# A decoder step of windowed attention, gated linear attention and SwiGLU: mixed tiles kept in DRAM as single values, and split where the output projection reads them

## The chip, the core and the metric

The kernel runs on one core of a Trainium2 chip. The metric is the device time of one execution in microseconds (us); lower is better. The core's engines are TensorE (PE in the profile; PEld is its weight load), VectorE (DVE), ScalarE (ACT), GpSimd (POOL) and SyncE (SP). DMAs are issued by SP's queue and by POOL's.

## The reference, cut to what matters

2048 prompt tokens and 8 decode tokens of width 1024 go through one layer in float32:

```python
def finish(x, o_attn, o_gla, r_gla, gla_norm_g, w_o, ffn_norm_g, w_gate, w_up, w_down):
    g = rmsnorm(o_gla, gla_norm_g).reshape(N, T, GLA_WIDTH) * jax.nn.silu(r_gla)
    h = x + jnp.concatenate([o_attn, g], axis=-1) @ w_o
    z = rmsnorm(h, ffn_norm_g)
    return h + (jax.nn.silu(z @ w_gate) * (z @ w_up)) @ w_down
```

`o_attn` (512 columns) is the sliding-window attention with sinks, `o_gla` (512 columns) the gated linear attention. Their concatenation is what the kernel calls the mixed tile: 128 tokens by 1024 columns, 16 tiles.

## The kernel before

Products are exact to nearly float32: an operand is split into a high part (rounded to fp32r by ACT, line 91) and a low part (the rest, a subtraction, line 92), and `mm3` issues three matmuls (lines 103 to 105): high times high, high times low, low times high. `split` is the helper for both steps; its last argument moves the subtraction from DVE to another engine.

The work runs in five stages, one behind the other, and the tile framework orders the instructions of each engine by a simulated timeline; every engine then works through its own list strictly in order.

- Attention, about 0 to 415 us. For each of 16 blocks of 128 tokens `front`, `project`, `project_r` and `attend` make the normalised input, the projections and the attention output `o` [128, 512], transposed. At the end of `attend` (lines 390 to 392) `o` is split into `mo`, the high part on ACT, the low part on POOL, and SP stores both (512 KB) into `mix_d[b]`.
- Linear attention, about 415 to 755 us. For each pair of blocks `front_b` projects and `gla_b` runs the recurrence. At its end (lines 861 to 864) ACT scales the transposed result `ps_m` by the gain into the high part of `mob`, DVE makes the low part, and SP stores 512 KB into the other half of `mix_d[b]`. `mob` has one buffer.
- Output stage, about 755 to 990 us. Eight pieces of the output weights are loaded as `wro` into a ring of four buffers (tag `raw`, pool `c_raw`) and split into `WO`. Then for each tile `product` (lines 962 to 983) loads the mixed tile, both parts, straight into `mt` (1 MB, two buffers), and the residual row block into `h`; 48 matmuls (2 halves, 8 k, 3 each) make `ps_wo`, DVE adds them to `h` (line 576), SP stores `h`. `normalise` squares `h` on ACT, scales it on DVE into `z` (line 992), TensorE transposes `z` (8 transposes, line 997). After two tiles `operands` makes seven units (b and t and their differences), each split on ACT and DVE into `zhl`, which has three buffers, and stored by POOL's queue to `zc_d` (line 1017, 512 KB each). Tiles go 0, 4, 1, 5, 2, 6, 3, 7, 8, 12, ..., the decode tile third from last; in the text "the second tile" is the second of this list. While the first tiles run, the `raw` ring also takes the first weights of the next stage (`wrg`), which are split into `whl`.
- Gate and up products (about 1000 to 1879 us) and down products (to 2340 us), each in a two-level Strassen form.

The rings of two to four buffers tie the engines together: a unit may be cast into `zhl` only when the store three units earlier has landed, a `wro` load waits until the split of the load four earlier is done, and SP's queue starts its DMAs in order, so one that waits holds those behind it.

Of the kernel before, what the change touches and what calls it, by code (L numbers as in the profile page):

```python
# [20 lines left out]
P = 128  # L21
# [30 lines left out]
def hymba_kernel(ctx: ExitStack, tc: tile.TileContext, I, O, X=None, phases=3):  # L52
# [11 lines left out]
    nT_d = [dram.tile([P, 2, KD, 256], F32, name=f"nT_d{i}") for i in range(NB // 2)]  # L64
    mix_d = [dram.tile([P, 2, KD, P], F32, name=f"mix_d{i}") for i in range(NB)]
    lr_d = [dram.tile([16, 256], F32, name=f"lr_d{i}") for i in range(NB // 2)]
# [76 lines left out]
    with ExitStack() as ph:  # L143
# [192 lines left out]
        def attend(b):  # L336
# [36 lines left out]
            kts = (1,) if b == 0 else (0, 1)  # L373
            o = wl.tile([P, 512], F32, tag="o", name="o", bufs=1)
            ol = wl.tile([P, 512], F32, tag="ol", name="ol", bufs=1)
            lo, hi = slice(0, 64), slice(64, 128)
            for v, (rh, rl) in enumerate(((lo, hi), (hi, lo))):
# [11 lines left out]
                nc.vector.tensor_tensor(o[rh], po[rh], ol[rh], ALU.add)  # L389
            mo = wl.tile([P, 2, 512], F32R, tag="mo", name="mo", bufs=1)  # L390
            split(mo[:, 0], mo[:, 1], o, nc.gpsimd)
            nc.sync.dma_start(mix_d[b][:, :, 0:4, :], mo.bitcast(F32).rearrange("p s (c t) -> p s c t", c=4))

# [188 lines left out]
    with ExitStack() as ph:  # L582
# [166 lines left out]
        def gla_b(pp):  # L749
# [68 lines left out]
            for c in range(2):  # L818
# [39 lines left out]
                for hh in range(4):  # L858
                    hc = slice(hh * P, (hh + 1) * P)
                    nc.tensor.transpose(ps[:, hc], ob[:, hc], ident)  # L860
                mo = wl.tile([P, 2, 512], F32R, tag="mo", name="mob", bufs=1)
                nc.scalar.activation(mo[:, 0], ps, AF.Copy, scale=gg)
                nc.vector.scalar_tensor_tensor(mo[:, 1], ps, gg, mo[:, 0].bitcast(F32), ALU.mult, ALU.subtract)
                nc.sync.dma_start(mix_d[b][:, :, 4:8, :], mo.bitcast(F32).rearrange("p s (c t) -> p s c t", c=4))

# [73 lines left out]
    with ExitStack() as ph:  # L939
# [21 lines left out]

        def product(ti):
            n = P if ti < NB else ND
            h = hp.tile([P, D], F32, tag="h", name="h")
            if ti < NB:
                mt = mixp.tile([P, 2, KD, P], F32R, tag="mix", name="mt")
                nc.sync.dma_start(mt.bitcast(F32), mix_d[ti])
                nc.sync.dma_start(h, I["x_prompt"][0, ti * P:(ti + 1) * P, :])
            else:
                nc.sync.dma_start(h[:n], I["x_sample"].rearrange("n o d -> (n o) d"))  # L970
            for dh in range(2):
                cols = slice(dh * 512, dh * 512 + 512)
                ps = acc.tile([P, 512], F32, tag="acc", name="ps_wo")
                for k in range(KD):
                    if ti < NB:
                        mm3(ps, mt[:, 0, k], mt[:, 1, k], WO[:, 0, k, cols], WO[:, 1, k, cols], k == 0, k == KD - 1)
                    else:
                        for hl in range(2):
                            nc.tensor.matmul(ps[:40], mixdec[:, k], WO[:, hl, k, cols], start=k == 0 and hl == 0,
                                             stop=k == KD - 1 and hl == 1)  # L980
                add_h(h, n, dh, ps)
            nc.sync.dma_start(h_d[ti] if ti < NB else hdec_d, h[:n])
            return h
# [39 lines left out]
        def after(ti):  # L1023
# [5 lines left out]
            if j == 1:  # L1029
                operands(sb, mt, bs.pop((sb, mt)))  # L1030

        for i, ti in enumerate(tiles):
            if ti == NB or (ti % 8 < 4 and (ti // 8, ti % 4) not in bs):
                key = (1, 3) if ti == NB else (ti // 8, ti % 4)
                bs[key] = [bp.tile([P, 4, 132], F32, tag=f"b{q}", name=f"b{q}", bufs=2) for q in range(4)]
            hs[ti] = product(ti)
            if i:
                after(tiles[i - 1])
# [317 lines left out]
```

## Time and profile before

| | |
|---|---|
| median of 3 runs | 2338.44 us (2336.45 to 2340.04) |
| the profiled execution | 2342.2 us, span 2340.4 us |
| busy share of the span | PE 95%, PEld 82%, DVE 68%, ACT 40%, POOL 27% |
| mean granted TensorE clock | 0.975 |
| DMA | 364.56 MB, mean 156 GB/s |
| the chain that ended last | PE 70%, DVE 8%, DMA 8%, issue 7%, POOL 4%, ACT 2% |

A busy PE is a modelled figure: each matmul's record is longer than the distance to the next, so a PE without gaps in the timeline is at its pace, whatever the sum of the records. "Idle before" names what the engine waited for last. The chain of waits goes back from the last instruction, at each step to what released it.

### The profile page before, as it was taken

The page shows a single profiled execution, that of the slowest core. Times are in us where ns is not written, and L with a number is a line of the kernel's source. Part 1 is how long each engine was busy: PE and PEld are TensorE (multiplying, and loading weights), DVE is VectorE, ACT ScalarE, POOL GpSimd, SP SyncE. Part 2 cuts the span into 40 slices and gives each one's busy share as a digit, 9 for nine tenths or more (in the row PEclk, how much of TensorE's full clock was granted, in tenths as well). Part 3 has the DMA queues.
Part 4 walks back from the last instruction along what each step waited for, and adds up shares of the span by engine and source line. Part 5 has one row for each costly group of instructions (what it writes and reads, how often), then busy time and mean ns, then how long its engine had stood idle before and what let it go on. Part 6 is the DMA issues. An engine that isn't in the chain of part 4 may idle for free.

```text
span 2340.4 us, 34821 instructions
## 1 busy us (share of the span) xinstructions
PE 2229.1 (95%) x12649; PEld 1923.1 (82%) x12649; DVE 1589.9 (68%) x3236; ACT 946.7 (40%) x2120; POOL 629.6 (27%) x807
## 2 busy tenths in 40 slices
PE   8899998999996999589999999999999989999998
PEld 6788887788885788478888889999999958787887
DVE  6687887587876655546666666767666674848477
ACT  5667877343433332223323233333333243534342
POOL 2444544364463122301101010101111112222222
PEclk9999999899997999799999999999999999999999
DMA  6323435243222899773333338323333357878877
GB/s 218 122 91 113 132 107 167 87 145 105 91 82 85 259 323 307 243 285 122 112 91 110 93 111 345 109 91 100 96 95 109 129 156 176 211 166 212 191 177 267
DMA packets 204571, 364.56 MB, mean 156 GB/s; under 512 B 15063, under 2 KB 127968, under 8 KB 198368
## 3 DMA queue, kind: packets, MB, share of 16 engines
q1 hardware_dynamic: 167376, 258.79, 34.3%
q0 software_dynamic: 37024, 103.55, 17.2%
q8 instruction: 100, 1.64, 0.3%
q14 instruction: 71, 0.58, 0.1%
HBM read 211.08 MB, written 152.27 MB: 155 GB/s over the span
## 4 chain that ended last, share of the span: by engine, by line
PE 70%; DVE 8%; DMA 8%; issue 7%; POOL 4%; ACT 2%; SPq 0%; POOLq 0%; ACTq 0%; DVEq 0%
PE ps_b L104 7%; PE ps_b L103 7%; PE ps_b L105 7%; PE ps_a L103 5%; PE ps_c L104 5%; PE ps_a L104 5%; PE ps_a L105 5%; PE ps_c L103 5%; PE ps_c L105 5%; DMA zc_d_P<-zhl 4%; PE ps_d L103 3%; PE ps_d L104 3%; PE ps_d L105 3%; POOL bd L776 1%; DMA wr<-in_w_in_dram 1%
## 5 line engine op out<-in xcount | busy, mean ns | idle before, releaser
L104 PE MATMUL ps_b<-z,whl 128*128 128x258 f32 (+1 forms) x792 | 253.4, 320 | 0.0
L103 PE MATMUL ps_b<-z,whl 128*128 128x258 f32 (+1 forms) x792 | 253.1, 320 | 0.0
L105 PE MATMUL ps_b<-z,whl 128*128 128x258 f32 (+1 forms) x792 | 252.2, 318 | 0.0
L103 PE MATMUL ps_a<-z,whl 128*128 128x258 f32 (+1 forms) x528 | 170.0, 322 | 26.0 <-DMA z<-zc_d_P 26.0
L91 ACT CAST dm<-mr 128x384 fp32r<-128x384 f32 (+1 forms) x224 | 107.8, 488 | 180.3 <-PE ps_b L105 95.8
L104 PE MATMUL ps_a<-z,whl 128*128 128x258 f32 (+1 forms) x528 | 170.1, 322 | 0.0
L105 PE MATMUL ps_a<-z,whl 128*128 128x258 f32 (+1 forms) x528 | 169.8, 322 | 0.0
L104 PE MATMUL ps_c<-z,whl 128*128 128x258 f32 (+1 forms) x528 | 169.1, 320 | 0.0
L105 PE MATMUL ps_c<-z,whl 128*128 128x258 f32 (+1 forms) x528 | 168.9, 320 | 0.0
L103 PE MATMUL ps_c<-z,whl 128*128 128x258 f32 (+1 forms) x528 | 168.5, 319 | 0.0
L105 PEld LDWEIGHTS ps_b<-z,whl 128*128 128x128 f32 x792 | 148.8, 188 | 12.0
L103 PEld LDWEIGHTS ps_b<-z,whl 128*128 128x128 f32 x792 | 148.9, 188 | 11.8
L104 PEld LDWEIGHTS ps_b<-z,whl 128*128 128x128 f32 x792 | 148.8, 188 | 11.8
L92 DVE TENSOR_TENSOR dm<-mr,dm 128x384 fp32r<-128x384 f32 (+1 forms) x224 | 114.7, 518 | 64.2 <-ACT dm L91 64.2
L91 ACT CAST whl<-wrg 128x512 fp32r<-128x512 f32 x132 | 81.6, 620 | 151.2 <-PE ps_b L105 83.1
L776 POOL TENSOR_TENSOR bd<-E,qTb 64x128 f32<-64x128 f32 x224 | 120.8, 539 | 66.1 <-ACT E L764 52.6
L103 PEld LDWEIGHTS ps_a<-z,whl 128*128 128x128 f32 x528 | 100.4, 190 | 34.6 <-DMA z<-zc_d_P 26.5
L1194 POOL DMA_DIRECT2D md_d<-m x22 | 15.6, 710 | 391.8 <-DVE m L1157 378.7
L936 DVE TENSOR_TENSOR gu<-ps_c,gu 128x512 f32<-128x512 f32 (+1 forms) x130 | 77.8, 599 | 56.1 <-PE ps_c L105 55.5
L92 DVE TENSOR_TENSOR whl<-wrg,whl 128x512 fp32r<-128x512 f32 x132 | 90.9, 689 | 35.2 <-ACT whl L91 34.9
L103 PE MATMUL ps_wo<-WO,mt 128*128 128x512 f32 x256 | 102.7, 403 | 9.4 <-ACT WO L91 9.4
L104 PEld LDWEIGHTS ps_a<-z,whl 128*128 128x128 f32 x528 | 100.1, 190 | 8.1
(386 smaller groups left out, 6617.5 us busy)
## 6 DMA issues: line engine op xcount, KB each, us to landing
mr<-md_d SPq DMA_DIRECT2D x24, 1344.0 KB
zc_d_P<-zhl POOLq DMA_DIRECT2D x49, 512.0 KB, 8.1
wrg<-in_w_gate_dram SPq DMA_DIRECT2D x44, 512.0 KB
wrg<-in_w_up_dram SPq DMA_DIRECT2D x44, 512.0 KB
nT_d<-nT SPq DMA_DIRECT2D x16, 1024.0 KB
zT<-nT_d SPq DMA_DIRECT2D x8, 2048.0 KB
mt<-mix_d SPq DMA_DIRECT2D x16, 1024.0 KB
z<-zc_d_P SPq DMA_DIRECT2D x7, 2064.0 KB
```

The source lines that it names most:

```text
L91: nc.scalar.copy(h, src)
L92: (eng or nc.vector).tensor_tensor(l, src, h.bitcast(F32), ALU.subtract)
L103: nc.tensor.matmul(ps, lh, rh, start=start, stop=False, skip_group_check=more)
L104: nc.tensor.matmul(ps, lh, rl, start=False, stop=False, skip_group_check=more)
L105: nc.tensor.matmul(ps, ll, rh, start=False, stop=stop, skip_group_check=more)
L776: nc.gpsimd.tensor_tensor(bv[rows, :, h], eo, qo, ALU.mult)
L936: nc.vector.tensor_tensor(out, a, b, ALU.add)
L1194: nc.gpsimd.dma_start(md_d[sb][g][:, :, q, fp - GROUPS[g][0], :], src.rearrange("p (m t) -> p m t", m=4))
```

## The change

The mixed tiles are stored as single float32 values. `mix_d[b]` has half the size. In the attention stage the split of `o` is gone, `o` has two buffers, and SP stores it as it is (256 KB). In the linear-attention stage ACT's scaled copy is the tile itself, VectorE's low part is gone, `mob` has two buffers of half the size. In the output stage `load_tile` loads a tile (512 KB) into a buffer `mr` of the `raw` ring and splits it into `mt` with ACT and DVE; it is called one tile ahead of the product.

```diff
--- before.py
+++ after.py
@@ -62,7 +62,7 @@
 
     ext_d = dram.tile([8, 384], F32, name="ext_d")
     nT_d = [dram.tile([P, 2, KD, 256], F32, name=f"nT_d{i}") for i in range(NB // 2)]
-    mix_d = [dram.tile([P, 2, KD, P], F32, name=f"mix_d{i}") for i in range(NB)]
+    mix_d = [dram.tile([P, KD, P], F32, name=f"mix_d{i}") for i in range(NB)]
     lr_d = [dram.tile([16, 256], F32, name=f"lr_d{i}") for i in range(NB // 2)]
     vdec_d = dram.tile([ND, 512], F32, name="vdec_d")
     rdec_d = dram.tile([ND, 512], F32, name="rdec_d")
@@ -371,7 +371,7 @@
                 nc.gpsimd.tensor_tensor(St[:, :, k0:], St[:, :, k0:],
                                         den[:, hs].unsqueeze(2).to_broadcast([P, 4, nk]), ALU.mult)
             kts = (1,) if b == 0 else (0, 1)
-            o = wl.tile([P, 512], F32, tag="o", name="o", bufs=1)
+            o = wl.tile([P, 512], F32, tag="o", name="o", bufs=2)
             ol = wl.tile([P, 512], F32, tag="ol", name="ol", bufs=1)
             lo, hi = slice(0, 64), slice(64, 128)
             for v, (rh, rl) in enumerate(((lo, hi), (hi, lo))):
@@ -387,9 +387,7 @@
                     nc.tensor.matmul(po, vv[:, v], pT[:, 1], start=False, stop=kt == 1)
                 nc.scalar.copy(ol[rh], po[rl])
                 nc.vector.tensor_tensor(o[rh], po[rh], ol[rh], ALU.add)
-            mo = wl.tile([P, 2, 512], F32R, tag="mo", name="mo", bufs=1)
-            split(mo[:, 0], mo[:, 1], o, nc.gpsimd)
-            nc.sync.dma_start(mix_d[b][:, :, 0:4, :], mo.bitcast(F32).rearrange("p s (c t) -> p s c t", c=4))
+            nc.sync.dma_start(mix_d[b][:, 0:4, :], o.rearrange("p (c t) -> p c t", c=4))
 
         def decode_a():
             with ExitStack() as decs:
@@ -858,10 +856,9 @@
                 for hh in range(4):
                     hc = slice(hh * P, (hh + 1) * P)
                     nc.tensor.transpose(ps[:, hc], ob[:, hc], ident)
-                mo = wl.tile([P, 2, 512], F32R, tag="mo", name="mob", bufs=1)
-                nc.scalar.activation(mo[:, 0], ps, AF.Copy, scale=gg)
-                nc.vector.scalar_tensor_tensor(mo[:, 1], ps, gg, mo[:, 0].bitcast(F32), ALU.mult, ALU.subtract)
-                nc.sync.dma_start(mix_d[b][:, :, 4:8, :], mo.bitcast(F32).rearrange("p s (c t) -> p s c t", c=4))
+                mo = wl.tile([P, 512], F32, tag="mo", name="mob", bufs=2)
+                nc.scalar.activation(mo, ps, AF.Copy, scale=gg)
+                nc.sync.dma_start(mix_d[b][:, 4:8, :], mo.rearrange("p (c t) -> p c t", c=4))
 
         def decode_b():
             a = dp.tile([P, 2, ND], F32, name="a")
@@ -959,15 +956,20 @@
             if dh == 0:
                 nc.sync.dma_start(gBf, bcast_rows(I["ffn_norm_g"], D))
 
-        def product(ti):
+        def load_tile(ti):
+            h = hp.tile([P, D], F32, tag="h", name="h")
+            if ti == NB:
+                nc.sync.dma_start(h[:ND], I["x_sample"].rearrange("n o d -> (n o) d"))
+                return None, h
+            mr = craw.tile([P, 1024], F32, tag="raw", name="mr").rearrange("p (k t) -> p k t", k=KD)
+            nc.sync.dma_start(mr, mix_d[ti])
+            mt = mixp.tile([P, 2, KD, P], F32R, tag="mix", name="mt")
+            split(mt[:, 0], mt[:, 1], mr)
+            nc.sync.dma_start(h, I["x_prompt"][0, ti * P:(ti + 1) * P, :])
+            return mt, h
+
+        def product(ti, mt, h):
             n = P if ti < NB else ND
-            h = hp.tile([P, D], F32, tag="h", name="h")
-            if ti < NB:
-                mt = mixp.tile([P, 2, KD, P], F32R, tag="mix", name="mt")
-                nc.sync.dma_start(mt.bitcast(F32), mix_d[ti])
-                nc.sync.dma_start(h, I["x_prompt"][0, ti * P:(ti + 1) * P, :])
-            else:
-                nc.sync.dma_start(h[:n], I["x_sample"].rearrange("n o d -> (n o) d"))
             for dh in range(2):
                 cols = slice(dh * 512, dh * 512 + 512)
                 ps = acc.tile([P, 512], F32, tag="acc", name="ps_wo")
@@ -1029,11 +1031,15 @@
             if j == 1:
                 operands(sb, mt, bs.pop((sb, mt)))
 
+        ready = load_tile(tiles[0])
         for i, ti in enumerate(tiles):
             if ti == NB or (ti % 8 < 4 and (ti // 8, ti % 4) not in bs):
                 key = (1, 3) if ti == NB else (ti // 8, ti % 4)
                 bs[key] = [bp.tile([P, 4, 132], F32, tag=f"b{q}", name=f"b{q}", bufs=2) for q in range(4)]
-            hs[ti] = product(ti)
+            now = ready
+            if i + 1 < len(tiles):
+                ready = load_tile(tiles[i + 1])
+            hs[ti] = product(ti, *now)
             if i:
                 after(tiles[i - 1])
         after(tiles[-1])
```

The order of the instructions on ACT where the output stage begins, before (`mob` is the last mixed tile, `wro` a piece of the output weights, `whl` a unit of the next stage's weights, line 990 the square of `h`):

```order
L862 ACTIVATE mob<-ps_m,gg 128x512
L91 CAST WO<-wro 128x2x512 x8
L91 CAST whl<-wrg 128x512 x2
L91 CAST whl<-sy 128x512 x2
L91 CAST whl<-wrg 128x512 x2
L91 CAST whl<-sx 128x512
L990 ACTIVATE z,ss<-h 128x1024 x2
L1000 COPY b_8522<-ps_zT 128x4x128
```

and now:

```order
L860 ACTIVATE mob<-ps_m,gg 128x512
L91 CAST WO<-wro 128x2x512 x8
L91 CAST mt<-mr 128x1024 x3
L992 ACTIVATE z,ss<-h 128x1024
L91 CAST mt<-mr 128x1024
L992 ACTIVATE z,ss<-h 128x1024
L1002 COPY b_8465<-ps_zT 128x4x128
L91 CAST zhl<-b_8464 128x4x128
```

The first `mt` casts stand behind all eight casts of the weights; before, no cast of a mixed tile stood on ACT, and the `whl` casts that followed the weights have moved to the end of the stage. On SP the first `mr` loads stand behind the eight `wro` loads in the same way.

VectorE in the middle of the output stage, before, from the third to the seventh unit of the fifth pair of tiles (`zhl` from `t_` or `b_` is a unit, `z` the normalised tile, `h` the residual sum):

```order
L92 TENSOR_TENSOR zhl<-t_9518,zhl 128x4x128
L576 TENSOR_TENSOR h<-ps_wo,h 128x512
L92 TENSOR_TENSOR zhl<-t_9516,zhl 128x4x128
L576 TENSOR_TENSOR h<-ps_wo,h 128x512
L1000 COPY b_9435<-ps_zT 128x4x128
L110 TENSOR_SCALAR rs_v<-ss 128x1
L992 SCALAR_TENSOR_TENSOR z<-h,rs_r,gBf 128x1024
L92 TENSOR_TENSOR zhl<-t_9519,zhl 128x4x128
L92 TENSOR_TENSOR zhl<-b_9244,zhl 128x4x128
```

and now:

```order
L92 TENSOR_TENSOR zhl<-t_9494,zhl 128x4x128
L92 TENSOR_TENSOR whl<-wrg,whl 128x512
L92 TENSOR_TENSOR zhl<-t_9492,zhl 128x4x128
L574 TENSOR_TENSOR h<-ps_wo,h 128x512
L1002 COPY b_9408<-ps_zT 128x4x128
L92 TENSOR_TENSOR mt<-mr,mt 128x1024
L92 TENSOR_TENSOR zhl<-t_9495,zhl 128x4x128
L110 TENSOR_SCALAR rs_v<-ss 128x1
L92 TENSOR_TENSOR zhl<-b_9211,zhl 128x4x128
L994 SCALAR_TENSOR_TENSOR z<-h,rs_r,gBf 128x1024
```

The subtraction of a mixed tile (`mt`) now stands behind the fifth unit, and `z` of the later tile behind the sixth and the seventh unit, where it stood ahead of both. Now that is so in every pair; before, `z` stood behind the seventh unit in the first two pairs only.

## Rows read from the trace of the kernel before

**Rows 1.** Busy time by stretch of 100 us. Columns: stretch and its length, then busy us of PE, PEld, DVE, ACT and POOL with the instructions in brackets, granted TensorE clock as a share of full speed, DMA share, GB/s. The first stretch lies in the attention stage, the second in the linear-attention stage.

```profile
100.00:200.00 100.00, 100.00 (x598) 85.38 (x597) 83.42 (x222) 73.78 (x199) 46.43 (x45) 1.00 0.31 97
...
600.00:700.00 100.00, 96.35 (x658) 86.12 (x657) 76.50 (x177) 38.05 (x95) 58.38 (x86) 1.00 0.27 84
```

**Rows 2.** The same view in short stretches: the end of the linear-attention stage, and two in the middle of the output stage.

```profile
715.00:735.00 20.00, 14.29 (x84) 13.17 (x83) 19.69 (x46) 7.48 (x18) 14.82 (x25) 0.78 0.40 137
...
820.00:840.00 20.00, 20.00 (x98) 16.75 (x97) 10.83 (x18) 6.57 (x11) 4.84 (x7) 1.00 0.97 327
...
880.00:900.00 20.00, 20.00 (x98) 16.71 (x98) 9.94 (x16) 6.87 (x12) 6.53 (x9) 1.00 0.93 325
```

**Rows 3.** The chain of waits where the attention stage ends: start us, us, what.

```profile
411.67 0.71 DVE o L389
...
412.44 0.63 ACT mo L91
...
413.14 1.27 POOL mo L92
...
415.00 3.59 DMA lm<-in_c_lmask_dram
...
418.62 0.39 DVE lmask L634
```

**Rows 4.** ACT in order of time at the same place: start us, us, engine line op out<-in, count.

```profile
415.87 0.64 ACT L707 ACTIVATE Bt<-Bt 128x528 f32<-128x528 f32 x1
```

**Rows 5.** The instructions on the tiles mo (attention stage) and mob (linear-attention stage): count, duration ns min/median/max, first and last start us, forms.

```profile
L92 POOL TENSOR_TENSOR mo<-o,mo x16: 1262/1291/1480, 89.3 to 413.1; 128x512 fp32r<-128x512 f32 x16
...
L862 ACT ACTIVATE mob<-ps_m,gg x16: 667/670/692, 466.6 to 752.9; 128x512 fp32r<-128x512 f32 x16
L863 DVE SCALAR_TENSOR_TENSOR mob<-ps_m,gg,mob x16: 736/751/753, 469.1 to 753.6; 128x512 fp32r<-128x512 f32 x16
```

**Rows 6.** The chain of waits of the linear-attention stage, the rows of line 863 in it: the first and the last of the eight that stand there before 740 us.

```profile
469.08 0.75 DVE mob L863
...
732.18 0.65 DVE mob L863
```

**Rows 7.** The chain of waits at the end of that stage, and under it TensorE's last transposes of a mixed tile from the timeline.

```profile
749.53 3.27 DMA mix_d<-mob
752.88 0.70 ACT mob L862
753.60 0.76 DVE mob L863
754.38 3.53 DMA mix_d<-mob
757.98 0.60 SPq L956
...
751.11 1.26 PE L860 MATMUL ps_m<-ident,ob 128*128 128x128 f32 x4 [4.07 <-DVE ob L856]
```

**Rows 8.** The start of the output stage. The first two rows are the timeline of ACT, the third that of SP's DMA queue, the last two the splits of the output weights in the tile view (columns as in rows 5).

```profile
775.59 1.05 ACT L91 CAST WO<-wro 128x1024 fp32r<-128x1024 f32 x1 [0.31 <-DMA wro<-in_w_o_dram]
...
777.05 0.62 ACT L91 CAST whl<-wrg 128x512 fp32r<-128x512 f32 x1 [0.41 <-DMA wrg<-in_w_gate_dram]
...
772.75 3.13 SPq L1137 DMA_DIRECT2D wrg<-in_w_gate_dram  x2
...
L91 ACT CAST WO<-wro x8: 1044/1048/1057, 760.4 to 775.6; 128x1024 fp32r<-128x1024 f32 x8
L92 DVE TENSOR_TENSOR WO<-wro,WO x8: 1215/1224/1227, 761.4 to 777.1; 128x1024 fp32r<-128x1024 f32 x8
```

**Rows 9.** TensorE in order of time: the first product of the output stage, five groups of transposes of a normalised tile (line 997), and the first matmuls of the stage behind it. In brackets the idle time before, and what ended it.

```profile
761.46 0.79 PE L103 MATMUL ps_wo<-WO,mt 128*128 128x512 f32 x1 [9.09 <-ACT WO L91]
...
800.71 1.03 PE L997 MATMUL ps_zT<-ident,z 128*128 128x128 f32 x8
...
919.24 1.03 PE L997 MATMUL ps_zT<-ident,z 128*128 128x128 f32 x8
...
931.01 1.03 PE L997 MATMUL ps_zT<-ident,z 128*128 128x128 f32 x8
...
944.35 1.55 PE L997 MATMUL ps_zT<-ident,z 128*128 128x128 f32 x8 [3.49 <-DVE z L992]
...
968.11 1.03 PE L997 MATMUL ps_zT<-ident,z 128*128 128x128 f32 x8
...
1000.54 0.80 PE L103 MATMUL ps_a<-z,whl 128*128 128x512 f32 x1 [26.05 <-DMA z<-zc_d_P]
...
1006.24 0.40 PE L104 MATMUL ps_a<-z,whl 128*128 128x512 f32 x1
```

**Rows 10.** ACT in order of time: the cast of the seventh unit of the second and of the sixth pair of tiles.

```profile
845.86 0.62 ACT L91 CAST zhl<-b 128x512 fp32r<-128x512 f32 x1 [5.66 <-DMA zc_d_P<-zhl]
...
945.22 0.62 ACT L91 CAST zhl<-b 128x512 fp32r<-128x512 f32 x1 [2.94 <-DMA zc_d_P<-zhl]
```

**Rows 11.** DMA issues between 760 and 1000 us: out<-in, queue, count, KB each, median us to landing where the profile shows it.

```profile
zc_d_P<-zhl POOLq DMA_DIRECT2D x49, 512.0 KB, 8.1
...
mt<-mix_d SPq DMA_DIRECT2D x14, 1024.0 KB
```

**Rows 12.** VectorE's split of the values in the attention stage (columns as in rows 5).

```profile
L92 DVE TENSOR_TENSOR vp<-ks,vp x16: 259/286/1874, 33.7 to 382.2; 128x128 fp32r<-128x128 f32 x16
```

## The prediction

> **What bounds the kernel now.** I read the busy time by stretch first. In the attention stage TensorE has no idle time between 100 and 200 us, so work taken from ACT, POOL or VectorE there is hidden [rows 1]. In the linear-attention stage TensorE is still at 96 of 100 us with VectorE at 77 [rows 1], but at its end, from 715 to 735 us, VectorE is full (19.69 of 20 us) and TensorE is not [rows 2]. In the output stage both TensorE (20.00 of 20 us) and the DMA engines (0.97 and 0.93) are full [rows 2]. The timeline shows which comes first: from the transposes at 919.24 to those at 931.01 us is 11.77 us, one tile (48 matmuls and 8 transposes) [rows 9]. From 800.71 to 931.01 eleven tiles pass, 129.5 us at that pace, and 130.3 us go by: TensorE sets the pace, losing 0.8 us. After that it does lose: 3.49 us before 944.35, waiting for `z` on VectorE [rows 9]. That is the other limit showing. The seventh unit of a pair is cast at 845.86 us in the second pair and at 945.22 in the sixth [rows 10], 24.84 us per pair where TensorE needs 23.54: the ring of three `zhl` buffers, waiting for stores that land in 8.1 us [rows 11], falls behind by 1.3 us a pair until VectorE, which works in order, holds up `z` behind a unit.
>
> **The change, part by part.**
>
> *Attention.* Gone are 16 casts of 0.63 us on ACT [rows 3] and 16 POOL subtractions of 1.29 us [rows 5], 20.7 us of POOL, and half the stored bytes. While TensorE is full they cost nothing, and taking them away gives nothing; the cover holds until the stage's last blocks. I take -0.5 us. The far end is three subtractions no longer waited for, -3.9 us; a loss has no cause but the second buffer of `o`, which only loosens.
>
> *The border to linear attention.* Here the last split is on the chain: `o` is done at 412.38 (411.67 and 0.71), ACT's cast and POOL's subtraction end at 414.41, and SP, in order, loads the mask `lm` only behind the store of `mo`; VectorE waits for it until 418.62 [rows 3]. Without them SP issues at 412.4. What is late next is the gate's logarithm, ending at 416.5 [rows 4], with a cast of 0.63 us less ahead of it on ACT: no later than `lm`, then due at 416.6. **-2.0 us**, between 0 (something unseen is as late) and -2.0.
>
> *Linear attention.* 16 VectorE operations of 0.75 us go [rows 5], 11.9 us. Eight of them stand on the chain before 740 us [rows 6], some 5.8 us. The last two, 1.4 us, lie where VectorE is full [rows 2] and count whole. Of the other six, 4.4 us, I count a third, because TensorE at 96% [rows 1] is late next: -1.5 us. Together **-2.9 us**, between -1.4 and -11.9. The two loads of 1 MB that ran ahead in this stage go too; DMA is at 0.27 there [rows 1], so 0.
>
> *The end of linear attention.* The last cast into `mob` waits until 752.88 for the store of the one before (the single buffer), while its transposes began at 751.11 and take 1.26 us; then 0.76 us of VectorE, then the store, behind which the weight loads stand on SP [rows 7]. Without the wait (0.5), the VectorE operation and its handover (0.8) and with half a store to wait for at 757.98, the weights come **1.5 us** earlier. It is counted in the next step.
>
> *The start of the output stage.* This is the price. Before, both first mixed tiles lay in SBUF, and TensorE began at 761.46 as soon as the first weight piece was cast [rows 9], working while the others came in. Now `mr` needs a buffer of the `raw` ring. The ninth load of that ring was issued at 772.75, when the fifth piece had been split, and its cast ran at 777.05, after waiting for the DMA [rows 8]. Now the ninth load is the first `mr`. Taking off 1.5 us, it has landed at 775.6, just after the last weight cast ends on ACT (776.6 less 1.5); the cast has the shape of a weight cast, 1.05 us [rows 8], so TensorE starts at 776.7. VectorE's 1.22 us end at 777.9, when the fifth matmul needs the low part. TensorE starts from rest, and the next stage shows what that costs: from 1000.54 to 1006.24 thirteen matmuls take 5.7 us, where 13 at full pace (10.7 us for the 48 of a product, below) take 2.9 [rows 9]. So it is as if it began at 779.5. Two products of 10.7 us (11.77 less 1.03 for transposes) bring the first transposes at 801.0, the second at 812.8, where before they came at 800.71. **+12.1 us.**
>
> *The rest of the output stage.* From 800.71 to 968.11 TensorE lost 0.8 us, and then 5.4: from 931.01 there are 37.1 us for 7.2 (decode product, 32 matmuls), 21.4 (two products) and 3.1 (three groups of transposes). Per pair the DMAs carry seven units of 512 KB, two mixed tiles of 1024 KB [rows 11] and four rows of `h` of 512 KB, 7680 KB in 24.84 us; now 6656 KB, 13% less, or 21.5 us at the same rate, below TensorE's 23.54. So the ring should keep up, and the lost time return. Kept whole the loss is 6.2 us, gone it is 0; I keep 1.6, because in every pair `z` now stands behind the seventh unit on VectorE: **-4.6 us**. The split itself, 1.05 and 1.22 us per tile, lies on engines with 6.9 and 9.9 us of work in 20 [rows 2], and so do the seven `whl` units moved in from the start: 0 while they keep half their time free; without that cover a tile's 2.3 us would each delay a product. The end of the stage, from the last product to the next stage's first matmul at 1000.54, keeps its work: 0.
>
> The DMA loads halve from 1024 to 512 KB [rows 11], and I scale their time with their bytes. The Trainium skill (DMA: Bandwidth & Descriptors, Measured (HBM→SBUF, 128 partitions, SWDGE, issued from GpSimd)) says to batch DMAs to at least 1 MiB, since smaller ones reach less of the peak. By that rule the relief is under 13% and the loss stays, which would make the sum below +6.7; the rows show stores of 512 KB with the DMA engines full at 327 GB/s [rows 2], so I stay with the bytes.
>
> **Sum:** -0.5 - 2.0 - 2.9 + 12.1 - 4.6 = +2.1 us. The profiled execution took 2342.2 us with a span of 2340.4; it would take 2344.3. The median of the runs is 2338.44, so **2340.5 us**. No change is what a measurement cannot tell, within 0.2% or 4.7 us.
>
> **Rivals.**
>
> *Locked to the ring (slower).* If the ring keeps its 24.84 us per pair, VectorE's new order passes it on: `z` waits for the seventh unit, TensorE for `z`, and every pair after the first loses 1.3 us. It decides when the seventh unit of a pair comes more than about 9 us after the transposes of the earlier tile (845.86 was that late, and 945.22 far later). Price: 7.8 us for six pairs in place of the 1.6 kept, sum +8.3, **2346.7 us**. For it speaks that the DMA engines were full, against it the 13%.
>
> *The late start unpaid (slower).* TensorE bounds all that lies ahead, so that only the border's 2.0 us count, and half of the lost time stays: 12.1 - 3.1 - 2.0 = +7, **2345.4 us**.
>
> *VectorE was the limit (faster).* Every low part counts whole: -11.9 in linear attention, -2.0, -3.9 in attention, and the loss of 6.2 us comes back: 12.1 - 6.2 - 17.8 = -11.9, **2326.5 us**. The usual split of `vp` takes 286 ns and once took 1874 [rows 12], so a VectorE operation can be held up by about as long as a POOL operation lasts, and 20.7 us of POOL vanish. The Trainium skill (SBUF — State Buffer, Who interferes with whom) has the rule: a VectorE instruction with two SBUF inputs and a GpSimd instruction that reads SBUF lock each other out. By it this rival gains weight, and `vp` agrees. Against it stands TensorE without a gap [rows 1].
>
> *It does not do what it says.* The first casts of `mt` stand behind all eight weight casts on ACT, so the late start cannot be scheduled away. But the lists of both attention stages were reordered as well, which may move some 4 us either way.
>
> **How the numbers follow.** My forecast, within 4.7 us, has 0.46. The two slower rivals have 0.22 and 0.14, the faster one with lucky reorderings 0.18. So faster 0.18, same 0.46, slower 0.36. The range takes in the slower rivals with 4 us of reordering on the dearer, **2351**, and reaches half-way into the faster one, **2331**; about 1 in 10 lies beyond each end.
>
> **What would show it.** TensorE's first matmul of the output stage comes about 23.5 us after the last store of `mob` is issued, where it was 7.1 (754.38 to 761.46); `lm` issued within 0.2 us of the last `o`; in the output stage a period of 11.77 us between groups of transposes, no idle time of TensorE above 1 us waiting for `z`, and DMA share near 0.87. Wrong would be: idle time of TensorE in every second tile, ended by `z` (the first rival), or a linear-attention stage shorter by 8 us or more (the third).

## The result, and the profile after

The changed kernel takes 2345.78 us (median of 6 runs, 2344.11 to 2349.19) beside 2337.44 us of the kernel before (6 runs, 2334.45 to 2342.55): ratio 1.0036, 95% interval 1.0024 to 1.0048. On another chip, in the run after2 below, the ratio was 1.0030 (1.0021 to 1.0038). So the change is slower by 0.3%, some 7 to 8 us. The predicted 2340.5 us was too low by 5.3. The time lies within the range of 2331 to 2351, but beyond the 4.7 us within which I had called it no change (0.46); what happened is the case to which I gave 0.36.

One trace is not enough here: the two profiled executions first compared lie 1.9 us apart, the medians 8.3. So both kernels were profiled a second time. The table cuts the four traces at the same marks of TensorE (the first mark is VectorE's last `o`); all times are us, "to" means from the mark above.

| mark | before, before2 | change, after2 | difference of the means | forecast |
|---|---|---|---|---|
| last `o` of attention | 411.67, 413.26 | 416.02, 416.41 | +3.75 | -0.5 |
| to the first `ps_l` (border) | 19.65, 18.74 | 17.67, 17.67 | -1.5 | -2.0 |
| to the last `ps_m` (linear attention) | 319.79, 320.13 | 313.47, 316.26 | -5.1 | -2.9 |
| to the second transposes of the output stage | 49.60, 51.48 | 59.75, 59.90 | +9.3 | +12.1 |
| to the last transposes but one | 167.40, 165.20 | 161.31, 161.31 | -5.0 | -4.6 |
| to the first `ps_a` | 32.43, 33.15 | 34.60, 37.49 | +3.3 | 0 |
| to the end | 1339.86, 1338.94 | 1339.38, 1339.56 | +0.1 | 0 |

The spans are 2340.4 and 2340.9 us before, 2342.2 and 2348.6 after; the differences add up to their +4.75. Two rows that I had near zero cost 7 us together.

The end of the attention stage in the changed kernel: TensorE's waits for `mx` (the row maximum that VectorE takes of the scores), from its timeline, then the last `o` on VectorE, then the load of the mask on SP's queue.

```profile
368.02 0.39 PE L354 MATMUL ps_s<-kT,qT 128*128 128x256 f32 x1 [1.59 <-DVE mx L359]
...
371.03 0.58 PE L354 MATMUL ps_s<-kT,qT 128*128 128x256 f32 x1 [2.27 <-DVE mx L359]
...
390.22 0.39 PE L354 MATMUL ps_s<-kT,qT 128*128 128x256 f32 x1 [3.02 <-DVE mx L359]
...
397.75 0.39 PE L354 MATMUL ps_s<-kT,qT 128*128 128x256 f32 x1 [0.99 <-DVE mx L359]
...
416.02 0.69 DVE L389 TENSOR_TENSOR o<-po,ol 64x512 f32<-64x512 f32 x1 [0.85 <-ACT ol L388]
...
417.18 0.37 SPq L631 DMA_DIRECT2D lm<-in_c_lmask_dram  x1
```

The border works nearly as forecast: `lm` starts 0.5 us after the end of the last `o` (416.71), where 2.6 us lay between them [rows 3]; the prediction had named 0.2 us as its sign. But `o` itself is late. TensorE waits 7.9 us for `mx` on the way, where its timeline in the kernel before shows one short wait for it behind 340 us:

```profile
369.41 0.39 PE L354 MATMUL ps_s<-kT,qT 128*128 128x256 f32 x1 [0.31 <-DVE mx L359]
```

All waits of TensorE from 340 us to the last `o` come to 11.9 us in both profiles of the change and to 8.9 and 7.7 us in those of before: 3.6 us more in the mean, about the +3.75 of the table.

The end of linear attention and the start of the output stage, timelines of TensorE, SP's queue, ACT and TensorE:

```profile
747.16 1.12 PE L858 MATMUL ps_m<-ident,ob 128*128 128x128 f32 x4 [3.41 <-DVE ob L854]
...
749.03 0.33 SPq L861 DMA_DIRECT2D mix_d<-mob  x1
...
764.99 8.49 SPq L965 DMA_DIRECT2D mr<-mix_d  x6
...
767.50 1.04 ACT L91 CAST WO<-wro 128x1024 fp32r<-128x1024 f32 x1 [0.28 <-DMA wro<-in_w_o_dram]
769.53 1.04 ACT L91 CAST mt<-mr 128x1024 fp32r<-128x1024 f32 x1 [0.99 <-DMA mr<-mix_d]
...
770.63 0.80 PE L103 MATMUL ps_wo<-WO,mt 128*128 128x512 f32 x1 [22.36 <-ACT mt L91]
...
776.30 0.40 PE L105 MATMUL ps_wo<-WO,mt 128*128 128x512 f32 x1
```

These rows answer to [rows 7 to 9]. TensorE starts 21.6 us after the last store of `mob` (forecast 23.5, before 7.1), behind the ninth load of the ring, and its first 13 matmuls take 5.7 us (770.63 to 776.30), as [rows 9] had let me expect.

TensorE's transposes from the second to the last, and the first matmul of the next stage:

```profile
806.91 1.03 PE L999 MATMUL ps_zT<-ident,z 128*128 128x128 f32 x8
...
936.41 1.03 PE L999 MATMUL ps_zT<-ident,z 128*128 128x128 f32 x8
...
956.84 0.66 PE L999 MATMUL ps_zT<-ident,z 8*128 8x8 f32 x8
968.22 1.03 PE L999 MATMUL ps_zT<-ident,z 128*128 128x128 f32 x8
975.19 1.94 PE L999 MATMUL ps_zT<-ident,z 128*128 128x128 f32 x8 [5.94 <-DVE z L994]
...
1002.82 0.79 PE L103 MATMUL ps_a<-z,whl 128*128 128x512 f32 x1 [25.68 <-DMA z<-zc_d_P]
```

From 806.91 to 936.41 eleven tiles pass in 129.5 us, 11.77 each, and nothing waits for `z` until the last group. The DMA engines have room, a share of 0.87 where the same stretch had 0.94 before, at 318 GB/s (columns as in rows 1):

```profile
800.00:900.00 100.00, 100.00 (x476) 83.52 (x475) 62.89 (x94) 36.51 (x60) 30.77 (x37) 1.00 0.87 274
```

Then the tail. VectorE's timeline, with two of ACT's casts for the last-but-one set of units between: the first unit that is a difference (from a `t`), and the seventh.

```profile
946.32 0.69 DVE L930 TENSOR_TENSOR sy<-wrg,sx 128x512 f32<-128x512 f32 x1
...
948.96 1.27 DVE L92 TENSOR_TENSOR whl<-wrg,whl 128x512 fp32r<-128x512 f32 x2
...
956.49 0.62 ACT L91 CAST zhl<-t 128x512 fp32r<-128x512 f32 x1 [5.75 <-issue]
...
969.71 0.62 ACT L91 CAST zhl<-b 128x512 fp32r<-128x512 f32 x1 [1.79 <-DMA zc_d_P<-zhl]
...
970.36 0.69 DVE L92 TENSOR_TENSOR zhl<-b,zhl 128x512 fp32r<-128x512 f32 x1 [1.72 <-ACT zhl L91]
970.97 0.68 DVE L574 TENSOR_TENSOR h<-ps_wo,h 128x512 f32<-128x512 f32 x1
...
973.76 1.28 DVE L994 SCALAR_TENSOR_TENSOR z<-h,rs_r,gBf 128x1024 f32<-128x1024 f32 x1 [0.74 <-POOL rs_r L111]
```

The same cast, and the last `h`, in the kernel before:

```profile
952.81 0.62 ACT L91 CAST zhl<-t 128x512 fp32r<-128x512 f32 x1 [1.87 <-issue]
...
968.31 0.69 DVE L576 TENSOR_TENSOR h<-ps_wo,h 128x512 f32<-128x512 f32 x1 [0.17 <-PE ps_wo L105]
```

The `whl` work for the next stage now stands here, so the first of these casts comes 0.35 us ahead of the decode tile's transposes (956.84), where before it came 3.70 us ahead of them (952.81 and 956.51). The casts behind it wait for stores, the seventh unit is late, and the last `h` and with it the last `z` stand behind that unit on VectorE.

### The profile page after: what moved, and what is told of

Read it like the earlier page. It is cut to its first block, busy times and chain, and to the rows that moved or that the text cites. A ratio compares the mean times of both kernels' runs of the same rounds, so it can differ in the third digit from the quotient of the medians.

```text
span 2342.2 us, 34794 instructions
## 1 busy us (share of the span) xinstructions
PE 2219.9 (95%) x12649; PEld 1918.2 (82%) x12649; DVE 1597.6 (68%) x3236; ACT 957.3 (41%) x2120; POOL 616.7 (26%) x791
## 4 chain that ended last, share of the span: by engine, by line
issue 50%; PE 28%; POOL 11%; DMA 4%; DVE 4%; ACT 2%; SPq 1%; POOLq 0%; ACTq 0%; DVEq 0%
POOL md_d L1200 5%; POOL h_d L1293 3%; PE ps_d L103 2%; PE ps_d L105 2%; PE ps_d L104 2%; PE ps_wo L103 2%; PE ps_wo L104 2%; PE ps_wo L105 2%; POOL bd L774 1%; DMA wr<-in_w_in_dram 1%; PE ps_v L105 1%; PE ps_v L103 1%; PE ps_v L104 1%; PE ps_p L382 1%; PE ps_l L779 1%
## 5 line engine op out<-in xcount | busy, mean ns | idle before, releaser
L105 PEld LDWEIGHTS ps_b<-z,whl 128*128 128x128 f32 x792 | 148.9, 188 | 11.9
L103 PEld LDWEIGHTS ps_a<-z,whl 128*128 128x128 f32 x528 | 100.5, 190 | 34.2 <-DMA z<-zc_d_P 26.1
L91 ACT CAST whl<-sx 128x512 fp32r<-128x512 f32 x88 | 54.6, 621 | 128.1 <-PE ps_b L105 63.5
```

Of the source, the lines that this page charges most:

```text
L91: nc.scalar.copy(h, src)
L103: nc.tensor.matmul(ps, lh, rh, start=start, stop=False, skip_group_check=more)
L105: nc.tensor.matmul(ps, ll, rh, start=False, stop=stop, skip_group_check=more)
```

## The experiments

All ratios are to the kernel before, run beside the others on the same chip; 0.001 is 2.3 us.

**before2.** The kernel before, unchanged.

> The kernel before once more, for a second profile. The two profiled executions so far lie 1.9 us apart where the medians lie 8.3 us apart. If the profiled execution of before (2342.2 us) was merely a long one, this one should be near the median, 2337 us, and the lost 4 to 5 us should be seen in one stage: the last o, the first ps_v, the last ps_m, the transposes of the output stage or the first ps_a then come 1 us or more earlier than 411.67, 414.17, 751.11, 968.11 and 1000.54. If each stage's times repeat within 0.5 us, the difference between profiled and unprofiled executions lies outside the stages that the change touches.

One run, 2342.76 us beside a median of 2341.78; the marks are in the table, within 2.9 us of the first profile. Neither expectation held in full: this execution was as long as the first, but on a chip whose median was higher.

**inplace.** The head start given back:

```diff
-            mr = craw.tile([P, 1024], F32, tag="raw", name="mr").rearrange("p (k t) -> p k t", k=KD)
-            nc.sync.dma_start(mr, mix_d[ti])
             mt = mixp.tile([P, 2, KD, P], F32R, tag="mix", name="mt")
+            mr = mt[:, 1].bitcast(F32)
+            nc.sync.dma_start(mr, mix_d[ti])
             split(mt[:, 0], mt[:, 1], mr)
```

> The change with one thing undone: a mixed tile is loaded straight into the low half of mt and split there, so it needs no buffer of the raw ring, and the first two tiles can be loaded before the weights. Theory of the late start: the first ps_wo comes one cast after the first weight piece (about 756 us, where the change has 770.6 and the kernel before 761.5), the second transposes about 25 us after the last weight cast, near 793.5 (change 806.9, before 800.7), the period stays 11.77 us, and the whole is 11 to 15 us shorter than the change: 2331 to 2335 us, ratio to before 0.997 to 0.999. Rival, the ring takes it back: the zhl ring and the DMA engines hold the pace again as in the kernel before, z is waited for at the end of the stage, and the gain is 4 to 8 us: 2338 to 2342 us. Rival, the start is not what costs (the time went elsewhere): within 2 us of the change, 2344 to 2348 us.

Ratio 0.9981 (0.9969 to 0.9992): 0.0052 below the mean of the change's two ratios, 12 us, as the first theory had it, and faster than the kernel before. The `whl` units go back to the start of the stage here, so this run undoes more than the late start; first2 tells the two apart. The start came 3 to 4 us later than expected, since linear attention ended later in this execution (last `ps_m` 750.01). TensorE's timeline:

```profile
759.38 0.80 PE L103 MATMUL ps_wo<-WO,mt 128*128 128x512 f32 x1 [8.11 <-ACT WO L91]
...
797.10 1.03 PE L999 MATMUL ps_zT<-ident,z 128*128 128x128 f32 x8
...
993.46 0.80 PE L103 MATMUL ps_a<-z,whl 128*128 128x512 f32 x1 [26.97 <-DMA z<-zc_d_P]
```

From the last `ps_m` to the second transposes it takes 47.1 us, against 59.8.

**first2.** Only the first two tiles are loaded in this way (`if ti in tiles[:2]`).

> The change with only its first two mixed tiles loaded straight into mt; the other 14 go through the raw ring as in the change, one tile ahead of the product, and the seven whl units stay among the tiles. Theory that the late start alone costs: start as in inplace (second transposes about 47 us behind the last ps_m; the change 59.7), ratio 0.997 to 0.9985. Theory that the moved whl units cost too, at the end of the stage: the start is won, but from the transposes of the last but one tile to the first ps_a it takes 34.5 us or more as in the change (inplace 33.5, before 32.4), and the ratio is 0.999 to 1.0.

Ratio 0.9991 (0.9980 to 1.0003). The start is won (46.0 us from the last `ps_m` to the second transposes), the tail is not:

```profile
957.85 1.09 PE L1002 MATMUL ps_zT<-ident,z 128*128 128x128 f32 x8
967.23 1.94 PE L1002 MATMUL ps_zT<-ident,z 128*128 128x128 f32 x8 [8.29 <-DVE z L997]
...
996.30 0.80 PE L103 MATMUL ps_a<-z,whl 128*128 128x512 f32 x1 [27.13 <-DMA z<-zc_d_P]
```

38.5 us from the last transposes but one to `ps_a`, against 33.5 in inplace, whose VectorE has none of the `whl` work in the stretch before. So the moved `whl` units cost by themselves, as the second theory says; in the ratios the two runs can't be told apart.

**dbl.** inplace with each tile loaded twice (`nc.sync.dma_start(mt[:, 0].bitcast(F32), mix_d[ti])` added), 8 MB more.

> The run inplace with the bytes of the mixed tiles doubled again: each tile is loaded twice, the second time into the high half, where the cast overwrites it. 8 MB more are read in the output stage; nothing else changes. Theory that the halved bytes are what freed the zhl ring: the DMA share goes back to about 0.93, z is waited for again in the second half, and it takes 2 to 6 us more than inplace, ratio 0.999 to 1.0005. Rival, the bytes did nothing and the order of the lists did: within 1 us of inplace, ratio 0.9975 to 0.9985.

Ratio 1.0018 (1.0008 to 1.0028), 8.7 us above inplace, more than the 2 to 6 expected; the second transposes to the last but one take 170.0 us, against 162.9. TensorE waits for `z` again, and the DMA share is back (timeline, and stretch as in rows 1):

```profile
948.48 1.06 PE L1000 MATMUL ps_zT<-ident,z 128*128 128x128 f32 x8 [3.93 <-DVE z L995]
...
800.00:900.00 100.00, 99.31 (x471) 81.79 (x470) 64.83 (x95) 38.46 (x61) 28.19 (x36) 1.00 0.93 312
```

The stores of `zhl` agree: their median to landing is 8.1 us before [rows 11], and, from the DMA views of the change, inplace and dbl:

```profile
zc_d_P<-zhl POOLq DMA_DIRECT2D x49, 512.0 KB, 6.1
```

```profile
zc_d_P<-zhl POOLq DMA_DIRECT2D x49, 512.0 KB, 6.6
```

```profile
zc_d_P<-zhl POOLq DMA_DIRECT2D x49, 512.0 KB, 7.2
```

This run does not hold everything else still: the lists of VectorE and ACT in the output stage differ from those of inplace too (the subtraction of `mt` stands later among the units of most pairs), and its linear attention took 319.7 us against 316.8. So the 8.7 us are not the price of the bytes alone.

**linkeep and low2.** VectorE's low part of `mob` put back, with one buffer (linkeep, shown) and with two (low2); the high part alone is stored:

```diff
+                mo = wl.tile([P, 2, 512], F32R, tag="mo", name="mob", bufs=1)
+                nc.scalar.activation(mo[:, 0], ps, AF.Copy, scale=gg)
+                nc.vector.scalar_tensor_tensor(mo[:, 1], ps, gg, mo[:, 0].bitcast(F32), ALU.mult, ALU.subtract)
```

> The change with the linear-attention half undone in its work: VectorE makes the low part of mob as before, mob has one buffer, and only the high part is stored, so the low part of that half is left out of the output. My sum had the 16 operations at 2.9 us and the wait for the store at 1.5 us: 4.4 us above the change, 2350 us, with the last ps_m near 750 instead of 747.2. Rival, VectorE was the limit there and all 11.9 us count: 2358 us. Rival, TensorE hides them: within 1 us of the change, 2346 us.

> The change with VectorE's low part of mob done again as dead work, but with two buffers of mob (the earlier run with one buffer came to 1.0068 of before, the change to 1.0036). It tells the VectorE operation from the wait for the store. If the operation itself is what counted: 6 to 8 us above the change, ratio 1.006 to 1.007, first ps_l to last ps_m about 321 us where the change has 313.5. If the single buffer counted: within 2 us of the change, ratio 1.003 to 1.0045, and about 314 us.

Ratios 1.0068 (1.0052 to 1.0085) and 1.0079 (1.0062 to 1.0095): 8 and 11 us above the change (each within some 4), of the operations' 11.9. Both lie above what was expected, 4.4 us by my sum and 6 to 8 us, though the 4 us of noise reach down to it (the profile of low2, which is its longest run, has 324.1 us for the stage). The second buffer brings nothing: the VectorE operation, with the lists that come with it, is what counts. linkeep, TensorE's first `ps_l` and last `ps_m`, 321.0 us apart:

```profile
433.85 1.95 PE L779 MATMUL ps_l<-bd,E 128*128 128x128 f32 x16
...
754.87 1.13 PE L858 MATMUL ps_m<-ident,ob 128*128 128x128 f32 x4 [4.08 <-DVE ob L854]
```

**attkeep, after2, attkeep2, dead.** Does attention lose by its new lists? In attkeep ACT and POOL split `o` as before and only the high part is stored; in dead the store of `o` stays as the change has it (the last two lines are not made). `o` has one buffer in both.

```diff
+            mo = wl.tile([P, 2, 512], F32R, tag="mo", name="mo", bufs=1)
+            split(mo[:, 0], mo[:, 1], o, nc.gpsimd)
-            nc.sync.dma_start(mix_d[b][:, 0:4, :], o.rearrange("p (c t) -> p c t", c=4))
+            nc.sync.dma_start(mix_d[b][:, 0:4, :], mo[:, 0].bitcast(F32).rearrange("p (c t) -> p c t", c=4))
```

> The change with the attention half undone in its work: o is split by ACT and POOL into mo as before (one buffer each), and only the high part is stored, so the low part of the attention half is left out of the output; bytes and everything behind it are as in the change. Theory that the reordered attention costs: the last o comes near 412 us instead of 416.0, the first ps_l 1.5 to 2.5 us earlier than 433.7, and the time is 1.5 to 4 us below the change, 2342 to 2344 us. Rival, the split on the path at the border costs its 2.0 us as my sum had it: 2 us above the change, 2348 us. Rival, neither counts: within 1 us of the change.

> The change once more, on the same chip as the next two, because its ratio (1.0036) and the ratio of attkeep (1.0002) were taken on different chips. If the reordered attention lists cost some 4 us, the ratio is 1.002 to 1.004 again and the last o comes at 415 to 416.5 us, as in the six executions with these lists so far. If the difference between the two lay in the chips, the ratio is 1.000 to 1.0015.

> The run attkeep again (o split in the attention stage, only the high part stored, so the low part of that half is left out of the output), now beside the change. Reordered lists cost: last o near 410 to 413 us and a ratio 0.0015 to 0.0035 below the change's of this call. No cost: within 0.001 of it. inplace_dead, which had these lists too, brought nothing against inplace, and its last o came at 415.2 us, so the first is the less likely now.

> The change with the split of o done again in the attention stage as dead work behind the store of o: nearly the lists of attkeep, and the border without a wait for the split. If attkeep's gain came from its lists, the ratio is that of attkeep2 or up to 0.001 lower. If storing half of mo instead of o made the difference, it is that of the change.

attkeep 1.0002 (0.9991 to 1.0012) and again 1.0002 (0.9993 to 1.0011), beside 1.0030 for the change on the chip of the second: with more work the kernel is 6.5 us faster. In the traces about 4 us of it lie ahead of the first `ps_l` (429.94 and 429.77, against 433.69 and 434.08), the rest in linear attention (311.8 and 311.2 us, against 313.5 and 316.3), which the edit does not touch; why was not traced. VectorE's last `o` in attkeep2, and the busy time from 350 to 400 us in the change and in attkeep2 (columns as in rows 1):

```profile
410.22 0.69 DVE L389 TENSOR_TENSOR o<-po,ol 64x512 f32<-64x512 f32 x1
```

```profile
350.00:400.00 50.00, 40.27 (x218) 33.68 (x218) 40.65 (x118) 36.67 (x98) 16.84 (x12) 0.86 0.53 172
```

```profile
350.00:400.00 50.00, 45.81 (x264) 38.45 (x263) 44.28 (x122) 38.19 (x101) 22.97 (x17) 0.90 0.51 169
```

TensorE is busy for 45.8 us in place of 40.3 at a granted clock of 0.90 in place of 0.86, and VectorE and ACT do more too. TensorE's waits from 340 us to the last `o` fall from 11.9 to 5.3 us, those for `mx` from 7.9 to 2.4. In seven executions with the change's lists the last `o` came at 415.05 to 416.41. dead came between, 1.0014 (1.0004 to 1.0024) with the last `o` at 412.8; why it falls short of attkeep was not settled.

**inplace_dead and inplace_copy.** inplace with the dead split as in dead, and inplace with ACT's copy of `o`, unrounded, stored as the value and POOL's subtraction kept as dead work.

> The mixed tiles loaded straight into mt as in the run inplace, and the split of o done again in the attention stage as dead work: the store takes o itself, nobody reads the split. It adds 20 us of POOL and 10 us of ACT to inplace and changes the lists of attention back nearly to those of the run attkeep. Theory that the new order of the lists costs: the last o comes between 410 and 413 us where the two kernels without the split have 415.6 and 416.0, TensorE's wait for mx behind 350 us shrinks from 7.9 us to under 3, and the two gains add up: ratio to before 0.995 (0.9981 and a third of a per cent less), 2326 us against 2337.4. Rival, the earlier end of attention came from the store of mo or is paid back at the border: ratio within 0.001 of inplace's 0.998. Rival, work counts: above 0.999.

> Both findings in one kernel: the mixed tiles loaded straight into mt (inplace, 0.9981), and ACT's copy and POOL's subtraction of o kept in the attention stage, the copy now unrounded and stored as the value, the subtraction dead. TensorE's list in the attention stage is that of attkeep. If attkeep's 0.0028 below the change and inplace's 0.0049 below it add up: ratio 0.994 to 0.9965, last o at 410 to 411 us. If, as in inplace_dead, the lists bring nothing here: 0.9975 to 0.999.

inplace_dead: 0.9983 (0.9972 to 0.9993), last `o` at 415.2; no gain, a miss for the theory in this form. Its list is shorter all the same. TensorE's timeline in dead and in inplace_dead, at its long wait in the first 100 us:

```profile
89.38 0.80 PE L103 MATMUL ps_d<-WR,nT 128*128 128x512 f32 x1 [6.43 <-ACT qs L288]
```

```profile
91.55 0.79 PE L103 MATMUL ps_d<-WR,nT 128*128 128x512 f32 x1 [7.81 <-ACT qs L288]
```

From this matmul to the last `o` it takes 323.2 and 324.1 us in the two profiles of before, 326.5 to 328.6 in the seven executions with the change's lists, 323.4 in dead, 323.7 in inplace_dead and 320.5 to 321.0 in attkeep, attkeep2 and inplace_copy. So `o` is late in inplace_dead because this execution was 2.2 us late by then; the attention behind it is 3.7 us shorter than in inplace (327.4). The border (20.0 us from the last `o` to the first `ps_l`, against 17.7) and the output stage (164.5 from the second transposes to the last but one, against 162.9) take it back. inplace_copy: **0.9954** (0.9941 to 0.9968), 2331.77 us beside 2343.98, faster than both kernels by its interval; the two findings add up. Last `o`, second transposes and first `ps_a`:

```profile
409.60 0.69 DVE L389 TENSOR_TENSOR o<-po,ol 64x512 f32<-64x512 f32 x1
```

```profile
793.09 1.03 PE L1002 MATMUL ps_zT<-ident,z 128*128 128x128 f32 x8
...
990.78 0.80 PE L103 MATMUL ps_a<-z,whl 128*128 128x512 f32 x1 [26.56 <-DMA z<-zc_d_P]
```

## Why the prediction was right or wrong, step by step

- **Attention, -0.5: wrong in sign, +3.75.** I priced the removed instructions and found them covered, which they were. The step that failed is the order: I named reordering of "some 4 us either way" beside the rivals, left it out of the sum, and looked at no row of it. attkeep, attkeep2 and inplace_copy show that the lists and not the work make the difference. Those of dead and inplace_dead bring 3 to 4 of the 6 to 7 us, counted from about 90 us on; which of their few differences from attkeep's counts stays open.
- **Border, -2.0: right,** -1.5.
- **Linear attention, -2.9: too small.** -5.1 in the traces, 8 to 11 us in the ratios of linkeep and low2. The failed step is the addition: -2.9 is 1.4 + 1.5, and the eight operations that I had read on the chain of waits, 5.8 us, are left out without a reason. With them the term is -8.7, inside what the ratios show. Whether "of the other six I count a third" was right as well, these runs can't tell: ten executions without the operation took 311.2 to 319.7 us here, four with it 319.8 to 324.1. TensorE at 96% did not hide the operations; the third rival is nearer to the ratios in this stage, and in this stage alone.
- **Start, +12.1: right in mechanism, 2.8 too dear.** TensorE came 21.6 and not 23.5 us after the store, because the weights came closer together: between the first and the last weight cast lie 12.9 us in the change, 15.2 before (754.63 to 767.50, 760.37 to 775.59). I had moved the old weight loads by 1.5 us unchanged. inplace and first2 show that this start is the largest single cost.
- **Rest of the output stage, -4.6: right,** -5.0; none of the loss was left. The cause that I gave, the bytes, is supported but not isolated: the DMA share fell, the stores landed sooner, and in dbl the wait for `z` comes back, but its lists differ as well. The first rival, the ring at 24.84 us a pair, did not occur. The Trainium skill (DMA: Bandwidth & Descriptors, Measured (HBM→SBUF, 128 partitions, SWDGE, issued from GpSimd)) wants batches of at least 1 MiB; by that rule the relief would have been lost on loads of 512 KB. This trace disagrees: with mixed tiles in loads of 512 KB the stores of 512 KB landed in 6.1 us in place of 8.1, and the lost time was won back.
- **Moved `whl` units and end of the stage, 0: wrong,** +3.3. I had the cover as ACT's and VectorE's free time in the middle of the stage. At its end such time does not help: between 961 and 971 us VectorE stands idle for 5.8 us behind ACT's casts, which wait for stores, and the last `h` and `z` stand in line behind these units. first2 and inplace differ there by 5 us.
- **The second rival's number, 2345.4, is nearly the time, its mechanism is not:** the lost time did come back, and not only the border counted.

The sum was +2.1. The traces say +4.75, the runs 7 to 8. That the sum came so near is partly luck: its terms miss by +4.25, +0.5, -2.2, -2.8, -0.4 and +3.3, and most of this cancels. What the last 3 us are is open: the change's first profile is its shortest run, and the table shows how two executions of one kernel differ by 3 us a row.

## What to carry to other kernels

Where a scheduler orders the lists, an instruction that is hidden is not free to remove: the lists move, and the price is read only from a trace of the new order. A prefetch that shares a ring with other loads starts when the ring lets it: put it where its data end up, as inplace does, and the head start stays. An operation that was read on the chain of waits belongs in the sum, whole, or with the reason why not. Price work that moves at the end of a stage by the queue that stands there, not by the busy share of its middle.

## What was not expected of the hardware

- The granted clock between 440 and 470 us was 0.89 in both profiles of before, in linkeep, low2, dead and after2, and 1.00 in the first profile of the change, attkeep, attkeep2, inplace, first2, inplace_dead and inplace_copy (0.94 in dbl). The same program thus had either, and from the first `ps_l` to the first `ps_m` it took 31.5 us in the one execution (433.69 to 465.23) and 34.3 in the other (434.08 to 468.36). Ahead of it TensorE had waited for `AT`: 2.12 us in the change's first profile, 2.41 in after2, 2.57 before. The length of this wait alone does not decide between the two levels (1.2 and 2.4 GHz): before2 waited 2.04 us and had 0.89, attkeep waited 2.30 and had 1.00. What does stays open. The rows, change and after2 (stretches as in rows 1, then the wait from each timeline of TensorE):

```profile
440.00:470.00 30.00, 27.61 (x181) 24.35 (x181) 18.12 (x45) 10.50 (x32) 9.48 (x15) 1.00 0.16 46
...
446.95 1.13 PE L779 MATMUL ps_l<-bd,E 128*128 128x128 f32 x8 [2.12 <-DVE AT L787]
```

```profile
440.00:470.00 30.00, 27.59 (x172) 25.26 (x171) 15.60 (x38) 9.03 (x26) 9.57 (x14) 0.89 0.13 37
...
447.62 1.30 PE L779 MATMUL ps_l<-bd,E 128*128 128x128 f32 x8 [2.41 <-DVE AT L787]
```

- The longest of VectorE's 16 splits of `vp` takes 1874 ns before [rows 12] and 1877 in attkeep2, and 1144 and 1139 in the two profiles of the change. The removed subtraction of `o` is not what holds it up. POOL's and VectorE's timelines in the kernel before:

```profile
108.35 1.89 POOL L371 TENSOR_TENSOR S<-S,den 128x1024 f32<-128x1024 f32 x1 [4.22 <-ACT r L238]
...
108.52 1.87 DVE L92 TENSOR_TENSOR vp<-ks,vp 128x128 fp32r<-128x128 f32 x1 [0.34 <-ACT vp L91]
```

It runs beside POOL's scaling of `S` (line 371) and ends with it, and the change keeps that instruction: in its first profile six of the 16 splits take over 0.6 us, two before. So what the third rival took as a sign for itself was not in what the change removes. The Trainium skill (SBUF — State Buffer, Who interferes with whom) lets a VectorE instruction with two SBUF inputs and a GpSimd instruction that reads SBUF lock each other out; this trace agrees, with 1.87 us for a split whose median is 0.29.
